# Normalising steps in a row behind the norm's factor, the wide form from tile pair 3 and conv triple 3, the first conv tap on ACT

## Chip, core and metric

One core of a Trainium2 chip runs the whole program. The metric is the device time of one execution in microseconds; lower is better. Engine names are those of the profile: PE (TensorE, matmuls), DVE (VectorE), ACT (ScalarE), POOL (GpSimd), SP (SyncE, which issues the loads).

## What is computed

Two layers of a residual trunk on 256 latent tokens of width 1024 (and 256 context tokens in the first layer). Each layer has three sub-layers; each normalises, scales and shifts its input, and adds its result back:

```python
def ffn_sublayer(h, m, g, w13, w2, base):
    hn = modulate(rms_norm(h, g), m[:, :, base], m[:, :, base + 1])
    return h + 0.5 * m[:, :, base + 2] * swiglu(hn, w13, w2)

def short_conv_mixer(h, w_in, conv_w, w_out):
    bg, cg, xin = jnp.split(h @ w_in, 3, axis=-1)
    z = cg * xin
    L = h.shape[1]
    zp = jnp.pad(z, ((0, 0), (1, 1), (0, 0)))
    y = zp[:, 0:L] * conv_w[0] + zp[:, 1:L + 1] * conv_w[1] + zp[:, 2:L + 2] * conv_w[2]
    return (bg * y) @ w_out
```

Layer 0 is feed-forward, a mixer of attention and pooling, feed-forward; layer 1 is feed-forward, the short convolution, feed-forward. `rms_norm` divides a token by the root of its mean square, `modulate` is `h * (1 + scale) + shift` with columns that come from the conditioning vector. All is float32.

## The kernel before

Activations lie transposed: 1024 channels are eight tiles (`d` or `k`, 0 to 7) of 128 partitions by 256 tokens, in `xl_all`. A float32 product is made from two parts of each operand, a rounded high one (`hi`) and the rest (`lo`). Weights come in chunks of 128 x 1024; ACT casts a chunk's high part (`whi`, L102) and DVE subtracts it from the chunk (`wlo`, L103). `Stream.get` does this three chunks ahead; four buffers hold split chunks, so a cast waits until PE has finished with the chunk four places earlier.

The stages that the change touches are the three feed-forwards behind the attention (function `ffn`, for layer 0 sub-layer 2, layer 1 sub-layers 0 and 2; in names `02`, `10`, `12`) and the convolution (`odd_mixer`, `11`).

A feed-forward multiplies into the hidden width in 22 tile pairs `f`, 0 to 21, each a pair of PSUM banks `pf` (`a` and `b` of the SwiGLU) drawn from three such pairs in turn (`ps2`); eight blocks `k` for each half. There are two forms.

- The **raw form** (`proj`, `mm3`, L252 to L254): the input times the norm's gain column, not yet divided by the root, stands in `ah`, with two more columns for the shift: 258 columns, three matmuls a block (high by high, high by low, low by high). It needs no norm's factor, so it can start at once. Its result is multiplied on DVE by the factor (`scaled`, L613, into a temporary `t...`, then SiLU with the shift as bias on ACT, L945, and L946).
- The **wide form** (`wide`, `mm2`, L259 and L260): the finished normalised input stands in `al` (high and low side by side, 512 columns), two matmuls a block of 512 and 256 columns. Its two halves are added by `joined` (ACT copy L621, DVE add L622).

The factor: squares are summed while the input is made; PE adds them over partitions (`pn`, L275), `root` takes the root on ACT and the reciprocal on DVE, `spread` (L298) transposes it over the partitions (PE L293) and copies it to `rs2` (ACT L300), with a dummy activation (L302) that loads the SiLU table.

A **normalising step** `act.normalise(d)` makes `al` for tiles d and d+1: product with the factor into a temporary `xn` (DVE L392), two ACTIVATEs with gain and shift (ACT L396), the high cast (ACT L401), the low subtraction (DVE L402). `xn`, the products of `scaled` and the sums of `joined` share one tag `t` with two buffers.

Before, pairs 0 to 3 are raw and 4 to 21 wide; a step is done ahead of the finish of each of pairs 0 to 3 (L980, L983). The convolution has eight triples `j`: a pair `pc` and a single bank `pb`, the same two forms (raw for 0 to 3), a step ahead of the finish of each of the first four, and a finish that makes `z`, three taps over it (L1029 the first, on DVE, and L1031 twice), the gate and the split of the result into `y2`. Its output projection (`OutProj`) does blocks k 0 to 6 of the outputs 0, 1 and 2 early (`pwo10` to `pwo12`), then their last block, then the other outputs.

Nothing writes out the order of these stages: the scheduler orders each engine's instructions by the program's order and the priority of `tc.high_priority`, and places buffers; `tc.issue_after(i)` keeps what stands in it behind instruction `i`. A wide group of PSUM needs all eight `k`; its `ks` argument allows parts, so the halves can take turns.

Of the kernel before, what the change touches and what calls it, by code (L numbers as in the profile page):

```python
# [20 lines left out]
KD = D // P  # L21
T = 256
# [18 lines left out]
CH = 8  # L41

OPERAND = 4160
F_RAW = 4
J_RAW = 4

C_MODB = 0
C_G = 144
# [71 lines left out]
def hybrid_trunk_kernel(ctx: ExitStack, tc: tile.TileContext, xc, cols_d, modw, wst, poolw_d,  # L120
# [141 lines left out]
    class Rstd:  # L262
# [34 lines left out]

        def spread(self):  # L298
            with tc.high_priority(offset=URGENT):
                nc.scalar.copy(rs2[:, self.q : self.q + self.n // T, 0:256], self.rows())  # L300
                if self.after is not None:
                    nc.scalar.activation(self.r[:, 4:5], self.r[:, 0:1], self.after)  # L302

    class Act:

# [632 lines left out]
    def ffn(act, l, s, gp, nxt_of, rate1, rate2):  # L938
# [15 lines left out]
        for f in range(NF):  # L954
            pt = pair(f"pf{l}{s}{f}")
            if f == 0:
                ws = W.get(), W.get()
                for ks in (range(KD - 1), range(KD - 1, KD)):
                    for h in range(2):
                        proj(pt, h, ws[h], act, (0,), ks)  # L960
                rr = act.rstd()
                held = pt
                continue
            if f == F_RAW:
                ws = W.get(), W.get()
                for ks in (range(KD - 2), range(KD - 2, KD)):
                    for h in range(2):
                        wide(pt[:, h, :], ws[h], act, ks)
            else:
                for h in range(2):  # L970
                    w = W.get()
                    if f == 1 and h == 0:
                        rr.root()
                    if f < F_RAW:
                        proj(pt, h, w, act, (0,), range(KD))
                    else:
                        wide(pt[:, h, :], w, act)
            if f == 1:
                rr.spread()
                act.normalise(0, gp)  # L980
                finish(0, held)
            if 1 <= f < F_RAW:
                act.normalise(2 * f, gp)  # L983
            finish(f, pt)
            if f >= F_RAW:
                mod_credit(rate1)
# [20 lines left out]
    def odd_mixer(act, gp, rate):  # L1007
# [7 lines left out]
        def finish(j, pt, pb):  # L1015
# [10 lines left out]
            else:  # L1026
                t = joined(pt, 2, gp, f"c{j}")
                nc.vector.tensor_tensor(z[:, 1 : T + 1], t[:, 0, :], t[:, 1, :], ALU.mult)
            nc.vector.tensor_scalar_mul(y, z[:, 0:T], cw[0])  # L1029
            for n in (1, 2):  # L1030
                nc.vector.scalar_tensor_tensor(y, z[:, n : n + T], cw[n], y, ALU.mult, ALU.add)  # L1031
            if j < J_RAW:
# [8 lines left out]
        for j in range(KD):  # L1041
            pt, pb = pair(f"pc{j}"), single(f"pb{j}")
            if j == 0:
                ws = W.get(), W.get()
                for ks in (range(KD - 1), range(KD - 1, KD)):
                    for h in range(2):
                        proj(pt, h, ws[h], act, (0,), ks)
                rr = act.rstd()
            elif j < J_RAW:
                for h in range(2):  # L1050
                    proj(pt, h, W.get(), act, (0,), range(KD))
            else:
                for h in range(2):
                    wide(pt[:, h, :], W.get(), act)
            w = W.get()
            if j == 0:
                rr.root()
            if j < J_RAW:
                for k in range(KD):
                    mm3(pb[:, 0:258], (w[0][:, k, :], w[1][:, k, :]), act.x(k, 0), k == 0, k == KD - 1)  # L1060
            else:
                wide(pb, w, act)
            if j == 0:
                rr.spread()
            if j < 4:
                act.normalise(2 * j, gp)
            finish(j, pt, pb)
            if j >= J_RAW:
                mod_credit(rate)
# [148 lines left out]
```

## Time and profile before

| what | value |
|---|---|
| time, median of 3 runs | 1175.89 us (1175.67 to 1176.23) |
| time of the profiled execution | 1177.64 us |
| its span | 1175.9 us |
| TensorE clock granted | 0.997 of full |
| stage of feed-forward `02`: first wide matmul, first of the second product | 544.9 us, 644.8 us |
| loads | 248.41 MB read, 212 GB/s over the span |

The span is the profiled stretch of an execution, the time is the whole of it. In the profile an engine's busy time counts instructions, and a row of the timeline reads: start in us from the span's start, duration in us, engine, line, operation, what it writes and reads, partitions by elements, count, and in brackets the idle time before it with what ended it. In the waits a row reads: who waited, for what, us in total, times, the longest.

### The profile page before, as it was taken

To read this page: it belongs to the slowest core of one execution; us is meant where nothing else is said; L and a number is where in the kernel's file an instruction comes from. 1 tells how busy PE (TensorE), PEld (TensorE's weight loads), DVE (VectorE), ACT (ScalarE), POOL (GpSimd) and SP (SyncE) were. 2 spreads that over 40 slices of the span, in tenths; PEclk is the share of its full clock that TensorE was granted. 3 is DMA by queue.
4 is the path that set the end of the run, shared out by engine and by line. 5 is a ranking of instruction groups with operands and counts; after the bars stand their busy time and mean duration, and the time that the engine had idled before them with its cause. 6 is when DMAs were issued, how large, how long until landed. Compare 5 with 4: busy or idle time off the path is not lost.

```text
span 1175.9 us, 16672 instructions
## 1 busy us (share of the span) xinstructions
PE 1145.7 (97%) x6479; PEld 984.7 (84%) x6479; DVE 926.0 (79%) x1487; ACT 576.0 (49%) x896; POOL 21.0 (2%) x23
## 2 busy tenths in 40 slices
PE   3999999999999999999999999999999999999997
PEld 2568888888888997889888889888889989988886
DVE  7976686587788687688888997988997988766654
ACT  4352322223243444567656547655546656655642
POOL 2000000000000040000000000000000000000000
PEclk9999999999999999999999999999999999999998
DMA  6773555366686764245687895787975554555551
GB/s 253 249 253 130 192 179 182 140 238 239 247 312 228 239 152 92 72 138 186 250 296 277 316 342 186 262 292 255 346 258 179 186 201 156 201 190 183 178 212 36
DMA packets 45791, 250.54 MB, mean 213 GB/s; under 512 B 12944, under 2 KB 13328, under 8 KB 17552
## 3 DMA queue, kind: packets, MB, share of 16 engines
q1 hardware_dynamic: 45712, 249.48, 60.9%
q8 instruction: 51, 0.84, 0.3%
q14 instruction: 28, 0.23, 0.1%
HBM read 248.41 MB, written 1.05 MB: 212 GB/s over the span
## 4 chain that ended last, share of the span: by engine, by line
PE 93%; DVE 2%; ACT 1%; DMA 1%; SPq 1%; issue 1%; DVEq 0%; ACTq 0%
PE pf L259 17%; PE pz L259 10%; PE pf L260 9%; PE pa L253 6%; PE pa L252 6%; PE pa L254 6%; PE pz L260 5%; PE p L564 4%; PE py L253 3%; PE py L252 3%; PE py L254 3%; PE pf L253 2%; PE pf L252 2%; PE pf L254 2%; PE pwo L259 2%; PE pc L259 1%
## 5 line engine op out<-in xcount | busy, mean ns | idle before, releaser
L102 ACT CAST whi<-raw 128x1024 fp32r<-128x1024 f32 x312 | 328.2, 1052 | 422.8 <-PE pa L253 114.1
L103 DVE TENSOR_TENSOR wlo<-raw,whi 128x1024 fp32r<-128x1024 f32 x312 | 380.7, 1222 | 162.8 <-ACT whi L102 162.0
L259 PE MATMUL pf<-al,whi 128*128 128x512 f32 x864 | 299.7, 391 | 0.0
L260 PE MATMUL pf<-al,wlo 128*128 128x256 f32 x864 | 241.9, 280 | 0.0
L203 DVE CUSTOM_DVE_ANT_0 jk<-mr,cvec,cols 128x1024 bf16<-128x1024 f32 x184 | 236.2, 1284 | 4.1 <-DMA mr<-in_modw 2.4
L259 PEld LDWEIGHTS pf<-al,whi 128*128 128x128 f32 x864 | 161.6, 187 | 35.3
L259 PE MATMUL pz<-g,whi 128*128 128x512 f32 x523 | 181.4, 391 | 0.0
L260 PEld LDWEIGHTS pf<-al,wlo 128*128 128x128 f32 x864 | 163.3, 189 | 0.0
L260 PE MATMUL pz<-g,wlo 128*128 128x256 f32 x523 | 146.4, 280 | 0.0
L259 PEld LDWEIGHTS pz<-g,whi 128*128 128x128 f32 x523 | 97.8, 187 | 21.4
L252 PE MATMUL pa<-xh,whi 128*128 128x512 f32 x288 | 112.0, 389 | 0.0
L254 PE MATMUL pa<-xh,wlo 128*128 128x512 f32 x288 | 112.0, 389 | 0.0
L253 PE MATMUL pa<-xl,whi 128*128 128x512 f32 x288 | 112.0, 389 | 0.0
L260 PEld LDWEIGHTS pz<-g,wlo 128*128 128x128 f32 x523 | 98.8, 189 | 0.0
L252 PE MATMUL py<-gh,whi 128*128 128x512 f32 x176 | 68.5, 389 | 0.0
L253 PE MATMUL py<-gl,whi 128*128 128x512 f32 x176 | 68.5, 389 | 0.0
L254 PE MATMUL py<-gh,wlo 128*128 128x512 f32 x176 | 68.5, 389 | 0.0
L252 PEld LDWEIGHTS pa<-xh,whi 128*128 128x128 f32 x288 | 54.1, 188 | 11.3
L254 PEld LDWEIGHTS pa<-xh,wlo 128*128 128x128 f32 x288 | 54.1, 188 | 11.2
L253 PEld LDWEIGHTS pa<-xl,whi 128*128 128x128 f32 x288 | 54.1, 188 | 11.2
L253 PE MATMUL pf<-ah,whi 128*128 128x258 f32 x192 | 54.5, 284 | 0.0
L252 PE MATMUL pf<-ah,whi 128*128 128x258 f32 x192 | 54.1, 282 | 0.0
(252 smaller groups left out, 1773.2 us busy)
## 6 DMA issues: line engine op xcount, KB each, us to landing
raw<-in_wst SPq DMA_DIRECT2D x156, 1024.0 KB, 5.0
mr<-in_modw SPq DMA_DIRECT2D x64, 1024.0 KB, 4.9
mr<-in_modw SPq DMA_DIRECT2D x16, 512.0 KB, 5.0
raw<-in_wst SPq DMA_DIRECT2D x8, 512.0 KB, 6.7
bias<-in_rpb SPq DMA_DIRECT2D x32, 64.0 KB, 5.8
xl_all<-in_xc SPq DMA_DIRECT2D x2, 512.0 KB, 8.3
xc_all<-in_xc SPq DMA_DIRECT2D x2, 512.0 KB, 9.7
out<-done SPq DMA_DIRECT2D x3, 256.0 KB, 2.7
```

What stands on the lines that cost most here:

```text
L102: nc.scalar.copy(hi, src)
L103: self.last = nc.vector.tensor_tensor(lo, src, hi.bitcast(F32), ALU.subtract).ins
L203: nc.vector.tensor_tensor_reduce(out=junk, in0=raw[:, h, :], in1=cvec[:, q, :], scale=1.0, scalar=cols[:, b : b + 1], op0=ALU.mult, op1=AL ...
L252: nc.tensor.matmul(out, wh, xh, start=first, stop=False)
L253: nc.tensor.matmul(out, wh, xl, start=False, stop=False)
L254: nc.tensor.matmul(out, wl, xh, start=False, stop=last)
L259: nc.tensor.matmul(out, wh, both, start=first, stop=False)
L260: nc.tensor.matmul(out[:, 0:256], wl, x[:, 0, :], start=False, stop=last)
L564: nc.tensor.matmul(pts[j], wf[:, j * P : j * P + P], f32, start=first, stop=last)
```

## The change

Pair 3 and triple 3 take the wide form (`F_RAW` and `J_RAW` from 4 to 3). In a feed-forward all four normalising steps stand behind `spread`, ahead of the finish of pair 0. In the convolution triple 0 has step 0, triple 1 steps 2 and 4, triple 2 step 6. The first wide pair of a feed-forward is made in three parts of `k` (four, two and two), the halves in turn, where it was two parts (six and two). The dummy activation that loads the table stands behind the copy of the factor. The first tap of the convolution is an ACTIVATE with the tap's column as scale. Behind L302 the changed kernel's line numbers are one higher.

```diff
--- before.py
+++ after.py
@@ -41,8 +41,8 @@
 CH = 8
 
 OPERAND = 4160
-F_RAW = 4
-J_RAW = 4
+F_RAW = 3
+J_RAW = 3
 
 C_MODB = 0
 C_G = 144
@@ -297,9 +297,10 @@
 
         def spread(self):
             with tc.high_priority(offset=URGENT):
-                nc.scalar.copy(rs2[:, self.q : self.q + self.n // T, 0:256], self.rows())
+                spread = nc.scalar.copy(rs2[:, self.q : self.q + self.n // T, 0:256], self.rows())
                 if self.after is not None:
-                    nc.scalar.activation(self.r[:, 4:5], self.r[:, 0:1], self.after)
+                    with tc.issue_after(spread.ins):
+                        nc.scalar.activation(self.r[:, 4:5], self.r[:, 0:1], self.after)
 
     class Act:
 
@@ -963,7 +964,7 @@
                 continue
             if f == F_RAW:
                 ws = W.get(), W.get()
-                for ks in (range(KD - 2), range(KD - 2, KD)):
+                for ks in (range(4), range(4, 6), range(6, 8)):
                     for h in range(2):
                         wide(pt[:, h, :], ws[h], act, ks)
             else:
@@ -977,10 +978,9 @@
                         wide(pt[:, h, :], w, act)
             if f == 1:
                 rr.spread()
-                act.normalise(0, gp)
+                for d in range(0, KD, 2):
+                    act.normalise(d, gp)
                 finish(0, held)
-            if 1 <= f < F_RAW:
-                act.normalise(2 * f, gp)
             finish(f, pt)
             if f >= F_RAW:
                 mod_credit(rate1)
@@ -1026,7 +1026,7 @@
             else:
                 t = joined(pt, 2, gp, f"c{j}")
                 nc.vector.tensor_tensor(z[:, 1 : T + 1], t[:, 0, :], t[:, 1, :], ALU.mult)
-            nc.vector.tensor_scalar_mul(y, z[:, 0:T], cw[0])
+            nc.scalar.activation(y, z[:, 0:T], AF.Copy, scale=cw[0])
             for n in (1, 2):
                 nc.vector.scalar_tensor_tensor(y, z[:, n : n + T], cw[n], y, ALU.mult, ALU.add)
             if j < J_RAW:
@@ -1062,8 +1062,8 @@
                 wide(pb, w, act)
             if j == 0:
                 rr.spread()
-            if j < 4:
-                act.normalise(2 * j, gp)
+            for d in ((0,), (2, 4), (6,))[j] if j < J_RAW else ():
+                act.normalise(d, gp)
             finish(j, pt, pb)
             if j >= J_RAW:
                 mod_credit(rate)
```

What the scheduler makes of it is shown at three places. Numbers in names are tiles of the program (`xn022`: step for tiles 2 and 3 in feed-forward `02`; `wlo97`: weight chunk 97; `tf020`: temporary of pair 0; numbers behind an underscore are the scheduler's).

DVE in feed-forward `02`, from the first step on, before:

```order
L392 TENSOR_TENSOR xn020_4333<-xl_all_99,rs2_97 128x512
L613 TENSOR_TENSOR tf020_4340<-pf020_4205,rs2_97 128x516
L103 TENSOR_TENSOR wlo96_4301<-raw48_4122,whi96_4300 128x1024
L946 SCALAR_TENSOR_TENSOR sl020_4339<-tf020_4340,sl020_4339 128x256
L402 TENSOR_TENSOR al02_4332<-xn020_4333,al02_4332 128x2x256
L392 TENSOR_TENSOR xn022_4346<-xl_all_99,rs2_97 128x512
L613 TENSOR_TENSOR tf021_4353<-pf021_4267,rs2_97 128x516
L952 TENSOR_TENSOR g02_0_4183<-sl020_4339,g02_0_4183 128x256
L103 TENSOR_TENSOR wlo97_4363<-raw48_4122,whi97_4362 128x1024
L402 TENSOR_TENSOR al02_4332<-xn022_4346,al02_4332 128x2x256
```

The same place of DVE in the changed kernel:

```order
L393 TENSOR_TENSOR xn020_4333<-xl_all_99,rs2_97 128x512
L393 TENSOR_TENSOR xn022_4339<-xl_all_99,rs2_97 128x512
L103 TENSOR_TENSOR wlo96_4301<-raw48_4122,whi96_4300 128x1024
L403 TENSOR_TENSOR al02_4332<-xn020_4333,al02_4332 128x2x256
L393 TENSOR_TENSOR xn024_4345<-xl_all_99,rs2_97 128x512
L103 TENSOR_TENSOR wlo97_4375<-raw48_4122,whi97_4374 128x1024
L403 TENSOR_TENSOR al02_4332<-xn022_4339,al02_4332 128x2x256
L393 TENSOR_TENSOR xn026_4351<-xl_all_99,rs2_97 128x512
L103 TENSOR_TENSOR wlo98_4403<-raw49_4206,whi98_4402 128x1024
L403 TENSOR_TENSOR al02_4332<-xn024_4345,al02_4332 128x2x256
L614 TENSOR_TENSOR tf020_4358<-pf020_4205,rs2_97 128x516
L103 TENSOR_TENSOR wlo99_4441<-raw49_4206,whi99_4440 128x1024
```

The product of pair 0 (`tf020`) stood second; now the steps' products and three of their subtractions and three weight subtractions stand ahead of it.

ACT at the same place, from the end of the norm on, before:

```order
L302 ACT_TABLE_LOAD
L302 ACTIVATE root0_120<-root0_120 128x1
L300 COPY rs2_97<-pn02_4264 128x256
L102 CAST whi96_4300<-raw48_4122 128x1024
L396 ACTIVATE xn020_4333<-xn020_4333,m02_106,g02_107 128x256 x2
L945 ACTIVATE sl020_4339<-tf020_4340 128x256
L401 CAST al02_4332<-xn020_4333 128x2x256
L102 CAST whi97_4362<-raw48_4122 128x1024
L951 CAST g02_0_4183<-sl020_4339 128x256
L396 ACTIVATE xn022_4346<-xn022_4346,m02_106,g02_107 128x256 x2
```

And in the changed kernel:

```order
L300 COPY rs2_97<-pn02_4264 128x256
L303 ACT_TABLE_LOAD
L303 ACTIVATE root0_120<-root0_120 128x1
L102 CAST whi96_4300<-raw48_4122 128x1024
L397 ACTIVATE xn020_4333<-xn020_4333,m02_106,g02_107 128x256 x2
L397 ACTIVATE xn022_4339<-xn022_4339,m02_106,g02_107 128x256
L402 CAST al02_4332<-xn020_4333 128x2x256
L397 ACTIVATE xn022_4339<-xn022_4339,m02_106,g02_107 128x256
L102 CAST whi97_4374<-raw48_4122 128x1024
L402 CAST al02_4332<-xn022_4339 128x2x256
L397 ACTIVATE xn024_4345<-xn024_4345,m02_106,g02_107 128x256 x2
L102 CAST whi98_4402<-raw49_4206 128x1024
```

The factor's copy moved ahead of the table load, and the SiLU and cast of pair 0 (L945, L951) moved behind the steps; the weight casts stay among them.

DVE in the convolution, around the end of the second triple's finish (`y1`), before:

```order
L103 TENSOR_TENSOR wlo232_8197<-raw116_7999,whi232_8196 128x1024
L1031 SCALAR_TENSOR_TENSOR y1_8151<-zpad1_7934,cols_84,y1_8151 128x256
L402 TENSOR_TENSOR al11_8035<-xn114_8254,al11_8035 128x2x256
L1034 SCALAR_TENSOR_TENSOR y1_8151<-tb1_8159,y1_8151 128x256
L103 TENSOR_TENSOR wlo233_8227<-raw116_7999,whi233_8226 128x1024
L1039 TENSOR_TENSOR y2_7931<-y1_8151,y2_7931 128x256
L613 TENSOR_TENSOR tc2_8262<-pc2_8164,rs2_97 128x516
```

In the changed kernel, from the subtraction of weight chunk 233 to that of the last step (`xn116`, tiles 6 and 7):

```order
L103 TENSOR_TENSOR wlo233_8203<-raw116_7969,whi233_8202 128x1024
L1031 SCALAR_TENSOR_TENSOR y1_8127<-zpad1_7904,cols_84,y1_8127 128x256
L393 TENSOR_TENSOR xn116_8230<-xl_all_99,rs2_97 128x512
L1031 SCALAR_TENSOR_TENSOR y1_8127<-zpad1_7904,cols_84,y1_8127 128x256
L103 TENSOR_TENSOR wlo234_8253<-raw117_8056,whi234_8252 128x1024
L1034 SCALAR_TENSOR_TENSOR y1_8127<-tb1_8135,y1_8127 128x256
L361 TENSOR_TENSOR ah12_8645<-m12_112,ah12_8645 128x8x2
L403 TENSOR_TENSOR al11_8005<-xn116_8230,al11_8005 128x2x256
```

The last step came after the product of triple 2 (`tc2`); now it stands within triple 1's finish, ahead of that product. On PE the last step is first asked for in triple 3 after six blocks of `pc3` and four of `pb3`.

PE at the early part of the convolution's output projection, from the last early block of output 0 on, before:

```order
L259 MATMUL pwo10_8703<-y2_7931,whi246_8622 128x512
L260 MATMUL pwo10_8703<-y2_7931,wlo246_8623 128x256
L259 MATMUL pwo11_8724<-y2_7931,whi246_8622 128x512
L260 MATMUL pwo11_8724<-y2_7931,wlo246_8623 128x256
L259 MATMUL pwo11_8724<-y2_7931,whi247_8644 128x512
L260 MATMUL pwo11_8724<-y2_7931,wlo247_8645 128x256
```

And in the changed kernel:

```order
L259 MATMUL pwo10_8649<-y2_7901,whi246_8568 128x512
L260 MATMUL pwo10_8649<-y2_7901,wlo246_8569 128x256
L259 MATMUL pwo12_8689<-y2_7901,whi247_8590 128x512
L260 MATMUL pwo12_8689<-y2_7901,wlo247_8591 128x256
L259 MATMUL pwo12_8689<-y2_7901,whi247_8590 128x512
L260 MATMUL pwo12_8689<-y2_7901,wlo247_8591 128x256
L259 MATMUL pwo11_8670<-y2_7901,whi246_8568 128x512
L260 MATMUL pwo11_8670<-y2_7901,wlo246_8569 128x256
```

Two blocks of output 2 moved ahead of the first block of output 1, which is the last to use weight chunk 246.

## The prediction

> **What bounds the kernel now.** I read the page's totals first, then the chain of work that ended last, then the waits of TensorE.
>
> ```profile
> span 1175.9 us, 16672 instructions
> PE 1145.7 (97%) x6479; PEld 984.7 (84%) x6479; DVE 926.0 (79%) x1487; ACT 576.0 (49%) x896; POOL 21.0 (2%) x23
> PE 93%; DVE 2%; ACT 1%; DMA 1%; SPq 1%; issue 1%; DVEq 0%; ACTq 0%
> PE pn L275 <- POOL sq L463: 10.7, 1, 10.7
> PE pwo L259 <- DVE xl_all L605: 2.1, 3, 1.1
> ```
>
> PE is busy for 97% of the span and makes up 93% of the last chain. Its longest wait (10.7 us) is at the start, ahead of all that changes. In the three feed-forward stages behind the attention no row of the waits names a `pf` or `pz` matmul. So in the changed stages a PE microsecond saved is a microsecond gained, and each wait put before a matmul is lost in full. DVE and ACT count only where PE would have to wait for them.
>
> **The change, part by part. 1: wide form one pair earlier.** Pair 3 of each feed-forward and triple 3 of the convolution go from three matmuls a block (258 columns each) to two (512 and 256). That is 16 blocks in each of three feed-forwards and 24 in the convolution: 72.
>
> ```profile
> 539.20 0.28 PE L252 MATMUL pf<-ah,whi 128*128 128x258 f32 x1
> 544.92 0.40 PE L259 MATMUL pf<-al,whi 128*128 128x512 f32 x1
> L259 PE MATMUL pz<-g,whi x523: 391/391/391, 644.8 to 1164.5; 128*128 128x512 f32 x175
> ```
>
> Durations of matmuls overlap, so I take distances of starts. Pair 3 is 48 matmuls from 539.20 to 544.92: 119.2 ns each, 357.5 ns a block. The 18 wide pairs run from 544.92 to the first `pz` at 644.8: 576 matmuls in 99.9 us, 173.4 ns each, 346.8 ns a block. The columns are nearly the same (774 and 768), so a block saves only 10.7 ns, and 72 of them **0.8 us**. Bounds: 0.7 to 0.9.
>
> **2: four normalising steps ahead of the first finish.** A pair's PSUM comes from three buffers, so pair 3 takes the one of pair 0. It may start when the product `tf` of pair 0 (L613, L614 after the change) has read it. Before, that product stood right behind the first step. Now four steps stand ahead of it on DVE, and both draw on the same two temporaries (tag `t`): the product can't start before the step for tiles 4 and 5 has ended. Here are the rows of before around the factor in the first of these stages.
>
> ```profile
> 529.56 0.38 PE L293 MATMUL pn<-ident,root 128*128 128x128 f32 x2
> 528.97 1.28 ACT L302 ACT_TABLE_LOAD   x1
> 530.37 0.35 ACT L300 COPY rs<-pn 128x256 f32<-128x256 f32 x1
> 530.70 1.05 ACT L102 CAST whi<-raw 128x1024 fp32r<-128x1024 f32 x1
> 531.66 1.09 ACT L396 ACTIVATE xn<-xn,m,g 128x256 f32<-128x256 f32 x2
> 532.65 0.49 ACT L945 ACTIVATE sl<-tf 128x256 f32<-128x256 f32 x1
> 533.05 0.60 ACT L401 CAST al<-xn 128x512 fp32r<-128x512 f32 x1
> 533.56 1.05 ACT L102 CAST whi<-raw 128x1024 fp32r<-128x1024 f32 x1
> 530.83 0.69 DVE L392 TENSOR_TENSOR xn<-xl_all,rs 128x512 f32<-128x512 f32 x1 [0.53 <-ACT rs L300]
> 531.44 0.69 DVE L613 TENSOR_TENSOR tf<-pf,rs 128x516 f32<-128x516 f32 x1
> 532.04 1.22 DVE L103 TENSOR_TENSOR wlo<-raw,whi 128x1024 fp32r<-128x1024 f32 x1
> 533.18 0.48 DVE L946 SCALAR_TENSOR_TENSOR sl<-tf,sl 128x256 f32<-128x256 f32 x1
> 533.68 0.69 DVE L402 TENSOR_TENSOR al<-xn,al 128x512 fp32r<-128x512 f32 x1
> ```
>
> From one start to the next (each overlaps its follower by about 0.09): table load with its dummy 1.40, factor copy 0.33, weight cast 0.96, pair of `xn` 1.00 (half 0.50), cast `al` 0.51; on DVE 0.61 for the 512-wide products, 1.14 for `wlo`. I lay them out in the order of the change, on the clock of before.
>
> ACT: the transposes end at 529.94, and the factor copy now stands ahead of the table load, so copy 529.98, load 530.31, weight cast 531.71, `xn` of step 0 532.67, half of step 2 533.67, cast `al` of step 0 534.17, the other half 534.68, weight cast 535.18, cast of step 2 536.14, `xn` of step 4 536.65, weight cast 537.65 to 538.70. DVE keeps up until there, then: `wlo` behind that cast 538.73, subtraction of step 4 539.87 to 540.56, and the product of pair 0, whose temporary that subtraction frees, 540.60 to 541.29. PE would be ready for pair 3 at 539.20, as before; it starts at 541.3. That is a **wait of 2.1 us**, three times alike (the three stages have the same order): **6.3 us**. Bounds for one: 1.6 if half a cast or handover overlaps better than the rows, 2.6 if each of some five handovers costs 0.1 more; both ends go into the range.
>
> Pair 3's own operands are in time: the last step's subtraction follows at about 542.4 to 543.1, and with six blocks of each half ahead, tiles 6 and 7 are asked for at 541.3 + 12 x 0.347 = 545.5. Behind the delayed product, pair 1's follows at about 543.4; pair 4 wants its buffer at 541.3 + 5.5 = 546.8. So the wait comes once a stage. That cover is 2.8 us; if it went, each further microsecond of lag would add one.
>
> The ACT/DVE work of pair 3's finish changes form (copy and add in place of the product), under a microsecond, hidden under PE's pairs of 5.5 us.
>
> **3: convolution, steps in rows of one, two and one, and the first tap on ACT.**
>
> ```profile
> 905.00:920.00 15.00, 15.00 (x128) 15.00 (x128) 14.63 (x26) 10.52 (x16) 0.00 (x0) 1.00 0.56 186
> L1029 DVE TENSOR_SCALAR y<-zpad,cols 128x256 f32<-128x256 f32 x8 | 2.8, 350 | 0.2
> L370 ACT ACTIVATE ah<-xl_all,g 128x256 fp32r<-128x256 f32 x32 | 16.2, 508 | 13.6 <-DVE xl_all L605 13.3
> 915.52 1.22 DVE L103 TENSOR_TENSOR wlo<-raw,whi 128x1024 fp32r<-128x1024 f32 x1
> 916.71 1.05 ACT L102 CAST whi<-raw 128x1024 fp32r<-128x1024 f32 x1 [0.67 <-PE pb L253]
> ```
>
> The windows row has DVE at 14.63 of 15 us here and ACT at 10.52. Eight taps leave DVE (8 x 0.35) and cost ACT 8 x 0.51 by the nearest row, a scaled ACTIVATE of the same size; they don't bound PE: 0 there. Each tap now crosses to ACT and back between two DVE rows, a delay, not work. The Trainium skill, page "ScalarE: Activation LUTs", section "Rules for kernel authors", advises VectorE rather than ScalarE for a multiply. By that page the tap loses time, and the two rows agree (508 against 350 ns), but since DVE is the full engine here and PE waits for neither tap, the sum is the same by both.
>
> What matters is the last step (tiles 6, 7), which triple 3 needs. In the new order PE does ten blocks of triple 3 (six of `pc3`, four of `pb3`) before it asks for tile 6: 10 x 0.347 = 3.5 us from its start, which is where the second triple's `pb` ends, 916.6 in before. On DVE eight rows run from `wlo` of weight 233 to the end of that step: 1.14 + 0.40 + 0.61 + 0.40 + 1.14 + 0.40 + 0.1 + 0.69 = 4.9 us. In before that `wlo` starts at 915.52, 1.1 us ahead of triple 3; from the same place the wait would be 4.9 - 1.1 - 3.5 = 0.3. The additional step ahead of it (1.3 us of DVE) less the tap (0.35) would push it to 1.25. Bounds 0 and 1.3; I take **0.6**, since DVE has some idle time to give.
>
> **4: end of the convolution.**
>
> ```profile
> 961.35 1.06 ACT L102 CAST whi<-raw 128x1024 fp32r<-128x1024 f32 x1 [1.40 <-PE pwo L259]
> 962.36 0.41 ACT L1038 CAST y<-y 128x256 fp32r<-128x256 f32 x1
> 962.79 1.28 ACT L160 ACT_TABLE_LOAD   x1
> 964.19 1.05 ACT L102 CAST whi<-raw 128x1024 fp32r<-128x1024 f32 x1
> 965.27 1.22 DVE L103 TENSOR_TENSOR wlo<-raw,whi 128x1024 fp32r<-128x1024 f32 x1 [1.27 <-ACT whi L102]
> 966.41 2.04 DVE L605 SCALAR_TENSOR_TENSOR xl_all<-pwo,m,xl_all 128x256 f32<-128x256 f32 x5
> 967.82 0.47 PE L259 MATMUL pwo<-y,whi 128*128 128x512 f32 x1 [0.84 <-DVE xl_all L605]
> ```
>
> This chain already makes PE wait 0.84 us: a weight cast that waits for PE to free its slot, the cast of `y`, a table load, a cast, `wlo`, the residuals. The new order puts two blocks of `pwo12` before the one of `pwo11` that frees the slot: 2 x 0.35 = 0.7 us later. Some 0.15 of it vanishes in an idle gap. Bounds 0.2 and 0.7; I take **0.55** more.
>
> **Sum.** -0.8 + 6.3 + 0.6 + 0.55 = **+6.65 us**. The profiled execution took 1177.64 (span 1175.9 and 1.7 around it) and would take 1184.3. The median shown, 1175.89, is 1.75 below that execution; the forecast is for the median: **1182.5**. A measurement of this kernel can tell about 0.2% (2.4 us) from no change.
>
> **Rivals.**
>
> *The waits don't come.* Pair 3 starts at 539.2 and only the 0.8 us remains: 1175.1, no slower than before. It decides on one row: the product of pair 0 must end by 539.2, 2.1 us earlier, as if two weight casts (0.96 each) stood behind the steps and not among them. Against it: the order as built has both among them, and ACT's rows are back to back. Chance 0.07.
>
> *The lag grows.* Pairs 4 and 5 wait again since finishes 0 to 2 and three weight pairs come in a crowd. Price: a second wait of 1 us in each stage, 1185.5. Point: pair 1's product later than 546.8, against 543.4 by the rows; 2.8 us of cover speak against it. Chance 0.05.
>
> *The clock falls in the waits.*
>
> ```profile
> 12.00:24.00 12.00, 3.04 (x12) 2.46 (x12) 11.36 (x18) 5.46 (x12) 5.50 (x4) 1.00 0.74 302
> ```
>
> Were PE to run at half rate for the first 16 matmuls behind each wait (2.77 us of work), each wait would cost 2.8 us more: 1190.8. The row is against it: the granted clock reads 1.00 in 12 us with PE busy for 3.04. The Trainium skill, page "TensorE: Matmul & The Clock Gate", Part 1, halves the clock after an idle window of about 3.4 us and restores it after a busy one. By that rule alone a wait of 2.1 us is too short to count on a fall, and if one came, an estimate from the page's window is 1.7 us a time, 1187.6; the row, with a longer idle stretch, shows no fall at all. Chance 0.03.
>
> **How the numbers follow.** Forecast 0.85, rivals 0.07, 0.05 and 0.03. With all low ends: -0.9 + 4.8 + 0 + 0.2 = +4.1, 1180.0; with all high ends: -0.7 + 7.8 + 1.3 + 0.7 = +9.1, 1185.0. I set 1179.5 to 1185.5, which takes in the growing lag too; the two other rivals lie outside. Slower by over 0.2% (above 1178.2): 0.85 + 0.05 + 0.03, less 0.02 for waits much shorter than my bounds: 0.91. Within 0.2%: that 0.02 and most of the first rival: 0.07. Faster: 0.02, the rest of that rival, if the existing waits went too.
>
> **What would show it.** Right: the waits of PE have a new row, `pf` L259 behind DVE `tf` L614, three times, about 2.1 us each and 6.3 in all; one before `pc` behind DVE `al` of about 0.6; `pwo` behind `xl_all` with a longest near 1.4 in the convolution; starts of pair 3's wide matmuls still 173 ns apart, clock 1.00. Wrong: no `pf` row in the waits (first rival), a second wait in each stage, a clock below 1.00 behind them, or a wait named for `al` or `wlo` rather than `tf`, which would say that the operand and not the buffer is late.

## The result, and the profile after

The changed kernel took **1192.59 us** (median of 6 runs, 1188.56 to 1197.96); the kernel before took 1176.74 beside it (6 runs). The ratio is 1.0137, 95% interval 1.0116 to 1.0157: slower, as forecast, but by 16 us where 6.65 were forecast, and outside the range. Three views of the changed kernel, each in the order in which the prediction read that of before. The page's totals and the chain:

```profile
span 1191.0 us, 16543 instructions
PE 1155.2 (97%) x6407; PEld 982.7 (83%) x6407; DVE 925.6 (78%) x1479; ACT 579.6 (49%) x908; POOL 21.1 (2%) x23
PE 88%; DVE 4%; ACT 3%; issue 1%; DMA 1%; SPq 1%; DVEq 0%; ACTq 0%
```

The profiled execution took 1192.81, its span is 15.1 us longer than that of before. Of these, 9.5 us are PE *busy* time, although the program has fewer matmuls. That is the part the prediction has no term for. The waits of PE:

```profile
PE pf L259 <- DVE tf L614: 6.2, 3, 2.1
PE pwo L259 <- DVE xl_all L606: 2.6, 3, 1.4
PE pc L259 <- DVE al L403: 0.4, 1, 0.4
```

These are the forecast waits: 6.3, the longest of `pwo` 1.4, and 0.6 were written. So the excess is not in the length of the waits. It begins right behind them. The timeline of PE around the wait in feed-forward `10`:

```profile
726.15 0.28 PE L254 MATMUL pf<-ah,wlo 128*128 128x258 f32 x1
728.50 0.58 PE L259 MATMUL pf<-al,whi 128*128 128x512 f32 x1 [2.07 <-DVE tf L614]
...
729.09 0.63 PE L259 MATMUL pf<-al,whi 128*128 128x512 f32 x1
...
729.74 0.63 PE L259 MATMUL pf<-al,whi 128*128 128x512 f32 x1
```

From 729.09 a block takes 0.65 us (to 729.74); the prediction's blocks take 0.347. The same stretches in windows (columns: window, its length, PE busy and count, granted clock, loads), laid so that the stretches at half clock fill one each:

```profile
537.59:541.00 3.41, 2.27 (x20) 1.00 0.60 171
541.00:544.42 3.42, 2.47 (x14) 1.00 0.60 177
...
725.32:728.74 3.42, 1.35 (x11) 1.00 0.84 304
728.74:732.15 3.41, 3.41 (x12) 0.50 0.48 139
...
1008.63:1012.04 3.41, 1.43 (x8) 1.00 0.61 255
1012.04:1015.45 3.41, 3.41 (x13) 0.50 0.84 281
```

**First excess: spells of half clock.** Behind the second and third wait the granted clock is 0.50 for 3.41 us, which loses 1.7 us each. The first wait, as long as the others, lies across the border of two windows (busy 2.27 and 2.47) and has none behind it. A third spell, from 469.3 on, lies in the attention, which the change doesn't touch; it is chance. The window ahead of it holds 1.55 us of PE work. In the kernel before, with windows of the same length counted from the start of its record of the clock, the same stretch falls into a window (from 466.65 on) with 1.72 us and has no spell.

**Second excess: a slower pace at full clock.** Windows of 80 us, L260's matmuls alone (one for each wide block), in the three feed-forwards of the changed kernel:

```profile
560.00:640.00 80.00, 63.93 (x231) 1.00 0.76 273
750.00:830.00 80.00, 63.91 (x232) 1.00 0.75 270
1030.00:1110.00 80.00, 63.54 (x228) 1.00 0.54 185
```

Two stages hold 231 or 232 blocks, as all three of before do (its third is the row below); the third holds 228.

```profile
1030.00:1110.00 80.00, 64.60 (x232) 1.00 0.55 186
```

By the distances of starts a block takes 346.7 ns in the first two and 353.4 in the third. With 304 blocks of `pf` and 176 of `pz` in a stage, a slow stage costs 480 x 6.7 ns = **3.2 us**. The convolution ran at 353.3 ns too, from 927.4 to 968.8, some 120 blocks: 0.8 us.

Together: -0.8 saved, 6.2 + 0.4 + 0.5 of waits, 3 x 1.7 of spells, 3.2 + 0.8 of pace: +15.4. The wait at the start (`pn`, 10.7 us before) is 9.1 here, long before the change begins: +13.8 against +15.1 measured. The other 1.3 us are spread over the span and have no term here.

### The profile page after: what moved, and what is told of

Same layout as the page of the kernel before. It is cut to its first block, busy times and chain, and to the rows that moved or that the text cites. A ratio compares the mean times of both kernels' runs of the same rounds, so it can differ in the third digit from the quotient of the medians.

```text
span 1191.0 us, 16543 instructions
## 1 busy us (share of the span) xinstructions
PE 1155.2 (97%) x6407; PEld 982.7 (83%) x6407; DVE 925.6 (78%) x1479; ACT 579.6 (49%) x908; POOL 21.1 (2%) x23
## 3 DMA queue, kind: packets, MB, share of 16 engines
HBM read 248.41 MB, written 1.05 MB: 209 GB/s over the span
## 4 chain that ended last, share of the span: by engine, by line
PE 88%; DVE 4%; ACT 3%; issue 1%; DMA 1%; SPq 1%; DVEq 0%; ACTq 0%
PE pf L259 18%; PE pz L259 10%; PE pf L260 9%; PE pa L254 5%; PE pa L253 5%; PE pa L252 5%; PE pz L260 5%; PE p L565 4%; PE py L254 3%; PE py L253 3%; PE py L252 3%; PE pwo L259 2%; PE pc L259 1%; DVE wlo L103 1%; ACT xn L397 1%
## 5 line engine op out<-in xcount | busy, mean ns | idle before, releaser
L259 PE MATMUL pf<-al,whi 128*128 128x512 f32 x912 | 321.5, 398 | 6.2 <-DVE tf L614 6.2
L260 PE MATMUL pf<-al,wlo 128*128 128x256 f32 x912 | 255.3, 280 | 0.0
L259 PEld LDWEIGHTS pf<-al,whi 128*128 128x128 f32 x912 | 172.7, 189 | 47.9 <-ACT whi L102 6.8
L260 PEld LDWEIGHTS pf<-al,wlo 128*128 128x128 f32 x912 | 173.1, 190 | 0.0
L260 PE MATMUL pz<-g,wlo 128*128 128x256 f32 x523 | 145.5, 278 | 0.0
L260 PEld LDWEIGHTS pz<-g,wlo 128*128 128x128 f32 x523 | 98.4, 188 | 0.0
L565 PE MATMUL p<-xn,raw 128*128 128x512 f32 x96 | 45.5, 626 | 2.7 <-ACT xn L483 2.7
L952 ACT CAST g<-sl 128x256 fp32r<-128x256 f32 x66 | 26.6, 402 | 36.5 <-DVE sl L951 31.7
```

The source lines that it names most:

```text
L259: nc.tensor.matmul(out, wh, both, start=first, stop=False)
L260: nc.tensor.matmul(out[:, 0:256], wl, x[:, 0, :], start=False, stop=last)
L565: nc.tensor.matmul(pts[j], wf[:, j * P : j * P + P], f32, start=first, stop=last)
L952: nc.scalar.copy(g2[f][:, 0, :], sl)
```

## The experiments

**Which half of the change.** Its feed-forward part alone:

```diff
-J_RAW = 3
+J_RAW = 4
-            nc.scalar.activation(y, z[:, 0:T], AF.Copy, scale=cw[0])
+            nc.vector.tensor_scalar_mul(y, z[:, 0:T], cw[0])
-            for d in ((0,), (2, 4), (6,))[j] if j < J_RAW else ():
-                act.normalise(d, gp)
+            if j < 4:
+                act.normalise(2 * j, gp)
```

> The feed-forward part of the change alone; the convolution as before. Theory A (a wait of PE costs more than its length: the wait itself, at times a spell of 3.4 us at half clock behind it, and at times a slower cadence of the wide matmuls behind it): waits of pf behind tf of 2.1 us three times, 0.5 us saved by the form, 0 to 3 spells at 1.7 us, wide blocks at 346.7 or 353.3 ns (3.1 us for a stage of 475 blocks): 1182 to 1196 us. Theory B (the excess over the forecast comes from the convolution and its end): 1182 us, all wide blocks of the feed-forwards at 346.7 ns, clock 1.00 behind the waits.

Measured 1188.66, ratio 1.0098 (1.0076 to 1.0121). The waits are there (6.2 us, 3 times, the longest 2.1, as above), spells stand behind the second and third wait, and this time the *first* stage is the slow one (228 blocks):

```profile
560.00:640.00 80.00, 63.55 (x228) 1.00 0.75 266
```

The convolution part alone (`F_RAW = 4`, steps and `spread` of the feed-forward as before):

> The convolution's part of the change alone; feed-forwards as before. Theory A: the only new waits are up to 0.6 us in triple 3 and 0.5 us more at the output projection, 0.25 us saved, and wide blocks of the convolution at 353.3 ns instead of 346.7 if that wait comes (1.2 us): 1176 to 1179 us, no spell at half clock in the feed-forwards and their wide blocks at 346.7. Theory B: 1184 us or more.

Measured 1176.73, ratio 1.000 (0.9991 to 1.001, 10 runs), no row for `pc` in the waits; `pwo` waits 2.7 in all where it waited 2.1 before. So the convolution part by itself is worth nothing that can be measured (the interval is -1.1 to +1.2 us); the loss is in the main the feed-forward's, 12.1 us of 15.9.

**The wait's cause.** Pair 0 is finished behind the first step, the other three steps follow:

```diff
-                for d in range(0, KD, 2):
-                    act.normalise(d, gp)
+                act.normalise(0, gp)
                 finish(0, held)
+                for d in range(2, KD, 2):
+                    act.normalise(d, gp)
```

> The whole change, but pair 0 is finished right behind the first normalising step, ahead of the three others, so its product no longer waits for a temporary. The wait of 2.1 us goes; one of about 0.4 us for tiles 6 and 7 takes its place in each feed-forward. Theory A: no spell at half clock behind so short a wait; if a short wait also draws the slower cadence, stages at 353.3 ns: 1177 to 1187 us; if not, 1177.5 us. Theory C (the denser order of ACT and DVE slows PE, not the wait): time stays near that of the change, 1188 us or more.

Measured 1185.78, ratio 1.0082 (1.0061 to 1.0103). No row of the waits names `pf` for `tf`, and no half clock in mid-span: it was the buffer that pair 3 waited for. But the time is still 9 us above before. In the trace pair 3 now loses, by the distances of starts, some 0.1 us ahead of tile 2 and 0.35 ahead of tile 4, whose subtractions on DVE end just before (the expectation had 0.4 for tiles 6 and 7), and two of three stages are slow (228, 231 and 227 blocks), of which the last:

```profile
1030.00:1110.00 80.00, 63.62 (x227) 1.00 0.54 186
```

**The wait without the earlier wide form** (`F_RAW = 4` in the changed kernel; pair 3 is raw and waits as long):

> The change with pair 3 of the feed-forwards in the raw form again; the four steps in a row stay, and so does the wait of 2.1 us ahead of pair 3, now before raw matmuls. Theory A in the form that the cadence is set where wide matmuls start behind a wait: wide blocks of all three feed-forwards at 346.7 ns again, spells at half clock as in the change: 1183 to 1189 us. If the cadence is drawn at the wait whatever follows, some stages stay at 353.3 ns: 1183 to 1197 us.

Measured 1186.76, ratio 1.008 (1.006 to 1.0099). Same wait, two spells, but all three stages fast (231, 231 and 232 blocks; the first is shown):

```profile
PE pf L252 <- DVE tf L614: 6.2, 3, 2.1
...
560.00:640.00 80.00, 64.64 (x231) 1.00 0.76 273
```

So spells go with the long waits, and the slow pace needs no long wait and isn't there where a whole raw pair stands between wait and wide blocks.

**No wait for the buffer** (feed-forward of the change; finish of pair 0 behind the third step; convolution as before):

```diff
+                act.normalise(0, gp)
+                act.normalise(2, gp)
+                act.normalise(4, gp)
                 finish(0, held)
+                act.normalise(6, gp)
```

> Feed-forwards in wide form from pair 3 as in the change, but the finish of pair 0 stands behind the third normalising step instead of the fourth, so that pair 3's banks come free in time; conv as before. Theory A (what the change lost is lost because TensorE stands still: the waits themselves, half-clock spells behind them, and a slower pace of the wide blocks that is drawn when they restart behind a wait): no wait of pf for tf, no spell in mid-span, every wide block at 346.7 ns, and 3 x 16 blocks x 10.7 ns = 0.5 us gained: 1176.0, ratio about 0.9996. Theory B (wide form so early, with the normalising steps beside it, is itself slower): wide stages at 353 ns without any wait, 1179 to 1183.

Measured 1181.72, ratio 1.0044 (1.0032 to 1.0057). No wait of `pf` in the list, no spell, yet two slow stages (232, 227 and 227 blocks). Theory A's number fell, and theory B's (1179 to 1183) holds here; the last run below decides against B. What the trace has is a gap of 0.26 us, by the distances of starts, ahead of pair 3's last blocks, whose operand DVE finishes just too late:

```profile
726.80 0.69 DVE L403 TENSOR_TENSOR al<-xn,al 128x512 fp32r<-128x512 f32 x1
```

Behind it the pace changes within one stage from 346.7 to 353.4 ns.

**Work in place of the wait.** Feed-forward part alone, with 20 matmuls that nothing uses:

```diff
                 ws = W.get(), W.get()
+                fill = single(f"fill{l}{s}")
+                for k in range(20):
+                    nc.tensor.matmul(fill[:, 0:258], ws[0][0][:, k % KD, :], act.x(k % KD, 0)[0], start=True, stop=True)
```

> The feed-forward part of the change alone (1188.7 when run before), with 20 matmuls of 258 columns into a free bank put ahead of pair 3's first wide matmul, so that TensorE works through the time in which it waited 2.1 us; their result is used by nothing. Theory A: the fillers cost 20 x 119.2 ns = 2.38 us in each feed-forward, 7.15 us, less 0.5 us of the wide form: 1183.2; no wait of pf for tf, no half-clock spell in mid-span, wide blocks at 346.7 ns in all three feed-forwards. Theory B (the excess comes of the order of the steps, not of TensorE standing still): 1188 to 1190, with slow stages as before.

Measured 1192.19, ratio 1.014 (1.0125 to 1.0156): a miss by 9 us. PE doesn't stand still, the clock has no spell in mid-span, and all three stages are slow from their first block on:

```profile
560.00:640.00 80.00, 63.58 (x227) 1.00 0.73 265
750.00:830.00 80.00, 63.63 (x227) 1.00 0.75 265
1030.00:1110.00 80.00, 63.59 (x227) 1.00 0.54 184
```

3 x 3.2 = 9.6 us is the miss. So the slow pace does not need a wait at all; the fillers had put the wide blocks into it.

**Two waits close together** (`F_RAW = 2` in the changed kernel):

> The change with the wide form from pair 2 instead of 3: pair 2 has to wait for the last normalising step and pair 3 for its banks. Two waits of about 2 us, half a microsecond of work apart, in each feed-forward. Theory A: 3 x 1.9 us more waiting less 48 x 10.7 ns = 5.2 us over the change, and a half-clock spell behind nearly every pair of waits (3 in a run and not 2, 1.7 us each): 1198 to 1203. Rival A2 (a spell needs one unbroken wait longer than some length near 2 us, the sum doesn't count): as many spells as the change or fewer, 1195 to 1198.

Measured 1200.43, ratio 1.0213 (1.0189 to 1.0237), within theory A's numbers. Waits and clock:

```profile
PE pf L259 <- DVE al L403: 10.5, 6, 1.9
...
534.56:537.97 3.41, 0.97 (x4) 1.00 0.16 65
537.97:541.39 3.42, 2.57 (x8) 0.50 0.58 196
```

Each of the three pairs of waits brings a spell, and each lasts two windows (6.83 us).

**Waits alone.** The kernel before, where a chain of GpSimd operations holds back the low half of a weight block:

```diff
+    def hold(lo, n):
+        src = lo.rearrange("p a b -> p (a b)")
+        nc.gpsimd.tensor_tensor(slow[:, 0:8], src[:, 0:8].bitcast(F32), zero[:, 0:8], ALU.mult)
+        while n > 0:
+            m = min(n, 256)
+            nc.gpsimd.tensor_tensor(slow[:, 0:m], slow[:, 0:m], zero[:, 0:m], ALU.add)
+            n -= m
+        nc.gpsimd.tensor_tensor(src[:, 0:8], src[:, 0:8].bitcast(F32), slow[:, 0:8], ALU.add)
...
+                    if h == 0 and (l, s, f) in DELAY:
+                        hold(w[1], DELAY[l, s, f])
```

> The kernel before, with nothing moved, but the low half of the weight block of pairs 6, 9, 12, 15 and 18 of each feed-forward is held back by a chain of GpSimd operations of different length (on values that it leaves as they are): 15 waits of TensorE between about 0.3 and 5 us, each in the middle of wide blocks. Theory A: half-clock spells of 3.4 us behind a part of the waits above 1 us and behind nearly all above 3.4 us, none behind waits under 1 us; the blocks that follow a wait run at 346.7 or at 353 ns until the next wait. Theory B (waits alone do nothing, it takes the moved normalising steps): no spell, all blocks at 346.7 ns, and the span longer than before by the sum of the waits alone.

Measured 1318.60, one execution. The chains ran longer than meant (1.1 us an operation on average), so the 15 waits were 4.5 to 10.5 us. Behind or within each stands half clock for one to four windows; 6 of the 15 stretches that follow went on at 353.4 ns, 9 at 346.7. Nothing of the change is in this kernel, so waits alone bring both. With shorter chains:

> The kernel before with 15 waits put in by GpSimd as in the first run of that kind, with shorter chains: waits of about 0.4 to 3.2 us (an operation of the chain took 1.09 us there). Theory A, with the clock read in windows of 3.413 us on a fixed grid: a window in which TensorE stands still for over 2.0 to 2.4 us is followed by one at half clock, whatever the length of the wait; waits that fall into two windows with less than 2 us in each, and all waits under 2 us, bring none. Rival (the length of the wait alone decides): all waits over some length bring a spell, wherever they lie on the grid. Pace: some of the 15 stretches at 353.4 ns, most at 346.7 (6 of 15 behind the long waits).

> The same again with other lengths, most of them 1.8 to 2.7 us, about that of the waits in the change. Theory A: of the waits near 2.1 us those that lie in one window of the grid are followed by a spell of 3.413 us, those cut by a window's edge with more than 0.3 us on either side aren't; by chance about (3.41 - 2.1) / 3.41 = 4 in 10 lie in one window whole, some more with nearly all of it. Rival (length alone): all or none of the waits between 2.0 and 2.3 us. Pace: as in the run before, a part of the stretches at 353.4 ns.

Measured 1202.89 and 1208.98, one execution each. Four waits of the first of the two (1.9, 1.9, 1.1 and 1.2 us) and two of the second (3.0 and 1.2 us). In each pair of rows the first is a window of the grid that holds the wait or most of it, the second the window behind it:

```profile
769.51:772.92 3.41, 1.52 (x9) 0.99 0.36 137
772.92:776.33 3.41, 3.41 (x12) 0.50 0.52 149
...
807.05:810.47 3.42, 1.55 (x9) 0.99 0.61 230
810.47:813.88 3.41, 3.41 (x13) 0.51 0.55 163
...
554.47:557.88 3.41, 2.35 (x14) 1.00 0.91 308
557.88:561.29 3.41, 3.41 (x21) 1.00 0.36 72
...
1035.75:1039.16 3.41, 2.80 (x17) 1.00 0.41 111
1039.16:1042.57 3.41, 2.86 (x16) 1.00 0.72 238
```

```profile
557.92:561.33 3.41, 1.40 (x8) 1.00 0.31 130
561.33:564.74 3.41, 3.41 (x13) 0.50 0.80 250
...
633.01:636.42 3.41, 2.26 (x13) 1.00 0.91 363
636.42:639.84 3.42, 3.42 (x21) 1.00 1.03 393
```

All spells of a run start on one grid of 3.413 us. A window in which PE was busy for 1.55 us or less is followed by one at half clock, a window with 2.26 or more is not; of the 21 waits in the two runs (12 and 9) none speaks against it. Theory A had laid the border at 2.0 to 2.4 us of standing still and no spell behind waits under 2 us; 1.9 us in one window were enough. As to the pace, five of the stretches behind waits of these two runs (0.15 to 3.1 us long) ran at 353.4 ns, most others at 346.7. Both runs fell short of the spread that was meant (waits of 1.8 to 2.0 us cut by a border are missing), so the rival of a mere length isn't excluded by them alone; the three waits of the change, all 2.07 to 2.08 us with one unlike the others, exclude it.

**What draws the pace.** The 20 fillers were of one form and ended on tile 3. Next, 7 raw groups of three:

```diff
+                fill = single(f"fill{l}{s}")[:, 0:258]
+                for k in range(7):
+                    mm3(fill, (ws[0][0][:, k, :], ws[0][1][:, k, :]), act.x(k, 0), True, True)
```

> As the run with fillers, but the fillers ahead of pair 3's first wide matmul are 7 groups of three in the very form of the raw pairs (high by high, high by low, low by high, 21 x 119.2 ns = 2.50 us a feed-forward). Theory C (the pace of wide blocks, 346.7 or 353.4 ns, is set by the timing in which the first of them follows what went before: behind raw matmuls in their own rhythm of 119, 115, 122, 119 ns it comes out at 346.7 each time, as in every stage of the kernel before; the other fillers left a different rhythm, and all three stages came out at 353.4): 3 x 2.50 - 0.5 = 7.0 over the kernel before, 1183.0, all three stages at 346.7 ns, no spell. Rival D (wide form from pair 3 with all four normalising steps beside it is slow whatever stands ahead): 353 ns again, 1192.

Measured 1192.18, ratio 1.013 (1.0113 to 1.0147); all three stages slow (228, 227 and 227 blocks). Theory C fell in the form in which it was put; rival D gave this number. And the version without the buffer wait, with two raw groups ahead of pair 4:

```diff
+                    if f == F_RAW + 1 and h == 0:
+                        fill = single(f"fill{l}{s}")[:, 0:258]
+                        for k in range(2):
+                            mm3(fill, (w[0][:, k, :], w[1][:, k, :]), act.x(k, 0), True, True)
```

> The run without the bank wait (1181.7), in whose trace pair 3 still waited 0.26 us for its last two tiles and two of three stages went on at 353.4 ns, with two raw groups of three (6 x 119.2 ns = 0.72 us a feed-forward, used by nothing) put ahead of pair 4. Theory C: the raw matmuls set the pace back to 346.7 ns in all three stages: 1176.0 - 0.5 + 0.8 (three short waits) + 2.15 = 1178.4. Rival D: slow stages stay, 1181.7 + 2.15 = 1183.9.

Measured 1186.72, ratio 1.0083 (1.0065 to 1.0102): inconclusive, since the scheduler put the fillers into pair 3, ahead of the late tiles, so that a wait, some 0.45 us by the distances of starts, again stood directly before wide blocks; two stages slow, one fast.

The distances of starts in the raw groups depend on the tile: 115, 122, 120 ns in the group of tile 7, 117, 123, 119 in that of tile 6. A raw pair ends on tile 7; the seven fillers ended on tile 6. So three more, each one step away from the run with seven:

```diff
-                for k in range(7):
+                for k in range(8):
```

> As the run with seven raw groups ahead of pair 3 (1192.2, three stages at 353.4 ns), with eight groups instead of seven, tiles 0 to 7, each group a start of its own: the last one is that of tile 7, as at the end of every raw pair. In the trace the raw matmuls' rhythm goes by the tile (tile 6: 117, 123, 119; tile 7: 115, 122, 120 ns), in pairs and fillers alike. Theory C1 (what stands directly ahead of the first wide matmul, a raw group of tile 7, sets 346.7 ns): three stages at 346.7 ns, fillers 3 x 24 x 119.2 ns = 8.6 us, less 0.5: 1184.4. Rival C2 (it is the accumulation over a whole pair, which fillers don't have) and rival D (four steps beside wide form): 353.4 ns again, 1193.5.

```diff
-                for k in range(7):
+                for k in range(1, 8):
```

> Seven raw groups ahead of pair 3 again, but of tiles 1 to 7 instead of 0 to 6: the number of matmuls is that of the run that came out at 353.4 ns, the last group is that of tile 7. Theory C1: three stages at 346.7 ns, 1183 to 1184. Rival (the number of matmuls, 21, puts the start out of step): 353.4 ns, 1192.

```diff
-                    mm3(fill, (ws[0][0][:, k, :], ws[0][1][:, k, :]), act.x(k, 0), True, True)
+                    mm3(fill, (ws[0][0][:, k, :], ws[0][1][:, k, :]), act.x(k, 0), k == 0, k == 6)
```

> Seven raw groups of tiles 0 to 6 ahead of pair 3, now accumulated in one bank (a start at the first, a stop at the last) as a pair does. Theory C1: tile 6 stands directly ahead, 353.4 ns in all three stages, 1192. Rival C2 (accumulation decides): 346.7 ns, 1183 to 1184.

Measured 1183.97 (ratio 1.0066, 1.005 to 1.0083), 1183.30 and 1192.26 (one execution each of the last two). Theory C1 gave all three. Starts of PE at the change of form, eight groups (tile 7 last), then seven (tile 6 last):

```profile
540.33 0.28 PE L254 MATMUL fill<-ah,wlo 128*128 128x258 f32 x1
540.45 0.40 PE L259 MATMUL pf<-al,whi 128*128 128x512 f32 x1
540.68 0.28 PE L260 MATMUL pf<-al,wlo 128*128 128x256 f32 x1
...
542.19 0.39 PE L259 MATMUL pf<-al,whi 128*128 128x512 f32 x1
```

```profile
542.07 0.28 PE L254 MATMUL fill<-ah,wlo 128*128 128x258 f32 x1
542.19 0.39 PE L259 MATMUL pf<-al,whi 128*128 128x512 f32 x1
542.42 0.28 PE L260 MATMUL pf<-al,wlo 128*128 128x256 f32 x1
...
543.95 0.40 PE L259 MATMUL pf<-al,whi 128*128 128x512 f32 x1
```

Five blocks take 1.74 us in the one and 1.76 in the other, and it stays so through the stage. Neither the number of matmuls nor accumulation decides; what stands directly ahead does.

**Without wait and without fillers.** The kernel before with `F_RAW = 3`, the later table load and the three parts of `k`, and:

```diff
-                act.normalise(0, gp)
                 finish(0, held)
-            if 1 <= f < F_RAW:
-                act.normalise(2 * f, gp)
+                with tc.high_priority(offset=URGENT):
+                    act.normalise(0, gp)
...
+                with tc.high_priority(offset=URGENT):
+                    act.normalise(6, gp)
```

> Feed-forwards in wide form from pair 3, conv as before, with the finish of pair 0 ahead of the steps and the four steps urgent, so that the product of pair 0, the banks of pair 3 and every tile should be ready when TensorE asks: no wait at all is meant to be new, and pair 3's first wide matmul stands directly behind a raw group of tile 7. By theory C1 and the waits: 48 blocks x 10.7 ns = 0.5 us gained and nothing lost, three stages at 346.7 ns, no spell behind pair 3: 1175.5 to 1176.0, ratio about 0.9996; where a short wait remains (under 0.3 us for tiles 4 to 7), a stage behind it can go to 353.4 ns and cost 3 us, 1178 to 1182. Rival D (wide form from pair 3 beside four steps is slow by itself): 353.4 ns in all three stages without any wait, 1184 to 1186.

Measured **1175.37** (11 runs, 1174.72 to 1176.54) beside 1175.86 for the kernel before (15 runs), ratio 0.9994 (0.9985 to 1.0003). No row of the waits names `pf`, no spell, three fast stages:

```profile
PE 1144.4 (98%) x6431; PEld 982.1 (84%) x6431; DVE 925.8 (79%) x1487; ACT 575.9 (49%) x899; POOL 21.2 (2%) x23
...
560.00:640.00 80.00, 64.60 (x232) 1.00 0.75 271
750.00:830.00 80.00, 64.60 (x232) 1.00 0.80 284
1030.00:1110.00 80.00, 64.60 (x232) 1.00 0.56 194
```

It is 17 us faster than the change and has, in the feed-forwards, its wide form and its four steps in a row (the convolution is as before), so rival D falls; against the kernel before the gain is the forecast size of the wide form and too small to be told from none.

## Why the prediction was right and wrong

**Right, term by term.** The wide form saves what was worked out: 0.5 us for the feed-forwards' 48 blocks, 1175.86 to 1175.37 in the last run (in size; the interval includes none). The wait for the buffer: 3 x 2.1 forecast, 6.2 found, named for `tf`; the run with pair 0 finished behind the first step takes it away by moving the finish alone. The product of pair 0 was laid at 540.6 with PE ready at 539.2; in the trace of the change it starts at 541.1, and PE, ready at 539.9, waits 2.08 us for it. `pc` 0.4 for 0.6, the end of the convolution 1.4 as written. The sign follows from these.

**Wrong: "each wait put before a matmul is lost in full".** It counted the length of a wait as its whole price. The runs show two further prices. A 2.1 us wait that lies mainly in one window brings 3.41 us of half clock, 1.7 us each: two of three in the profiled execution of the changed kernel, of its feed-forward part alone, and of the kernel with `F_RAW = 4`, 3.4 us each time. And wide blocks that start behind a wait, not behind the end of a raw pair, may run at 353.4 ns: 3.2 us a stage, none of which the prediction had. The forecast's +6.65 and these two (3.4 of spells, 0.8 in the convolution, and one or two slow stages) make 14 to 17 us over before; 15.9 were measured. How many spells and slow stages an execution draws is chance as far as these runs show: its six lie between 1188.56 and 1197.96.

**The rival that was nearest was dismissed on a row that showed nothing.** "The clock falls in the waits" had a chance of 0.03, since the granted clock read 1.00 in a window with PE busy for 3.04 of 12 us. The same stretch in the run of the feed-forward part alone (columns: PE, PEld, DVE, ACT, POOL, clock):

```profile
12.00:24.00 12.00, 3.92 (x13) 2.97 (x14) 11.23 (x21) 4.96 (x12) 4.03 (x3) 0.50 0.71 282
```

The clock there was at half. In the trace of before, the record of the clock begins only behind this stretch, at 29.7 us, and the window is printed as 1.00. Its matmuls say it. Two of 128 x 128 took 0.69 us in this window and 0.38 at 529.56, by the row in the prediction; 12 of another form, right behind the window and from 33.77 on:

```profile
19.27 0.69 PE L293 MATMUL pn<-ident,root 128*128 128x128 f32 x2 [0.55 <-DVE root L286]
24.59 7.96 PE L564 MATMUL p<-xn,raw 128*128 128x512 f32 x12 [2.74 <-ACT xn L482]
33.77 5.31 PE L564 MATMUL p<-xn,raw 128*128 128x512 f32 x12
```

The row against the rival was a row for it: the clock is at half in and behind a long idle stretch (PE waited 10.7 us there). Whether 2.1 us are enough, it couldn't say. The other estimate in that rival, 1.7 us a spell, is what was found. The rule on which it stood, in the Trainium skill, page "TensorE: Matmul & The Clock Gate", Part 1 (a window of 3413 ns that runs freely, half clock behind an idle one), agrees with the grid and the length here; but the window needn't be idle as a whole: 1.55 us of work in it did not keep the clock up.

**Too small to tell:** the convolution part was charged 0.9 us net; alone it came out 0.2 over before, and the interval takes in both 0.9 and none. The wait before `pc` isn't there alone; the longer one of `pwo` is (2.7 for 2.1).

**Open:** why the matmul directly ahead sets the pace of hundreds of blocks, and what picks it behind a wait. Fast and slow stages came behind long waits, short ones, and within one stage. The first and the second wait of the changed kernel left the fast pace, the third the slow one.

## What to carry to other kernels

A wait of an engine that is otherwise full costs more than its length: look at the granted clock and at the distances of starts in the whole stage behind it, not only at the idle time. Where an operation is moved ahead, ask first which buffer its neighbour was about to free: here the finish of pair 0 stood behind four steps, and with it ahead of them, and the steps made urgent, all of the loss was gone. And before a row is taken as evidence against a mechanism, see that the quantity was recorded there: a second sign (here the length of equal matmuls) takes a minute.

## What the hardware showed that was not expected

- The granted clock is decided on a fixed grid of 3.413 us. On the grid of each run, counted from a change of its clock, a window with PE busy for up to 1.56 us was followed by half clock, with one exception (1.54 us, in the first kernel with waits), and none with 1.68 or more was, if it ran at full clock itself. In the attention the same stretch fell into windows with 1.55 or 1.56 us in five runs, each with a spell behind it, and with 1.68 to 1.93 in seven, all without. Two waits in a row kept the clock down for two windows: in the first of them PE was busy for 2.57 us, at half rate, and the second was at half clock all the same.
- Pairs of matmuls of 512 and 256 columns have two steady paces at full clock, 346.7 and 353.4 ns, each held for hundreds of blocks. The feed-forward stages that began behind a raw group of tile 7 all began at the fast one; the nine that began behind a group of tile 6 or 20 equal fillers at the slow one.
- An operation of 128 x 256 on GpSimd took 1.12 us on average in the first chains, with a wide spread; the kernel before has 0.65 for some of this size and 1.05 for another.
